# One core's encoder block: another order in the opening, output weights split a stage earlier, one slot more in the recurrence

## The chip, the cores and the metric

The kernel runs on one core of a Trainium2 chip. A core has five engines with a queue of instructions each: TensorE (PE in the profile; its weight loads are listed as PEld), VectorE (DVE), ScalarE (ACT), GpSimd (POOL) and SyncE (SP, which here only issues DMAs; ScalarE issues some too). An engine runs its instructions in the order of its queue and waits at one whose input is not there yet. PE writes into PSUM, eight banks of 128 x 512 floats; the others read the banks and work in the core's memory, SBUF. The metric is the device time of one execution in microseconds (us), the median of several runs.

## The reference

One layer of a bidirectional encoder on 1024 tokens of width 1024, all in float32:

```python
h = layer_norm(x, ln_in_g, ln_in_b)
proj = h @ w_in[l]
aq, ak, av, hq, hf_fwd, hf_bwd, hi, hg, ga, gh = jnp.split(proj, split_idx, axis=-1)
att = dilated_attention(aq, ak, av, slopes)
rec = hgrn2(hq, hf_fwd, hf_bwd, hi, hg, lower_bounds[:, l], hgrn_norm_g[l])
merged = jax.nn.sigmoid(ga) * (att @ w_att_up[l]) + jax.nn.sigmoid(gh) * (rec @ w_hgrn_up[l])
h = layer_norm(DEEPNORM_ALPHA * h + merged @ w_o[l], ln1_g[l], ln1_b[l])
gate, up = jnp.split(h @ w_ffn_in[l], 2, axis=-1)
h = layer_norm(DEEPNORM_ALPHA * h + (jax.nn.silu(gate) * up) @ w_ffn_out[l], ln2_g[l], ln2_b[l])
```

The projection has 11,776 columns, the feed-forward 2 x 2,816. The recurrence `hgrn2` is a gated linear one with 8 heads of 128 in both directions, in chunks; the attention has 24 heads of 64 in three groups with different dilation.

## The kernel before

**Products.** Every float32 operand is split into a high part (a cast to PE's fp32r type, on ScalarE, L212) and a low part (operand minus high part, on GpSimd or VectorE, L222). A product is three matmuls, high x high, high x low and low x high (`mm3`, L268 to L272), of 128 x 128 weights and 512 columns. The projection and the feed-forward use a scheme of Winograd's form of Strassen's method: tokens and contraction are halved, and seven products (numbers 1, 2, 6, 5, 7, 3, 4 in this order) with sums of weight blocks (`a11` to `a22`, `s1` to `s4`) and of activation blocks take the place of eight. The activation blocks are called `b11`, `b21` (first four token tiles) and `t1`, `t2`, `t3`, `b22`, `t4` (which need the other four): `t1 = b12 - b11`, `t2 = b22 - t1`, `t3 = b22 - b12`, `t4 = b21 - t2`. One product of one group is 12 matmuls of 512 columns; this is a slot of the projection.

**The order.** A planner with a model of the engines' times puts the instructions of each engine in order when the program is built, by priority (program order, raised by `high_priority`) and by when it thinks operands are ready. `behind` and `ordered` add an order between two instructions by hand. SP's loads of weight blocks are in a chain of their own (`queued`).

**Opening (`phase0`, L316 to L488).** The eight token tiles of x are loaded; VectorE takes the statistics (`stats`), GpSimd ends them, ScalarE normalises each half of a tile (`norm`), PE turns it 128 columns at a time into a bank (`turn`, L364), and ScalarE and VectorE apply gain and bias and write the blocks (`scaled`, `less`, `hi`, `lo`). Between the steps `run` lets `stream` (L615) issue the next slot of the projection. Four banks, used in turn (`ps_sd`), serve the turned tiles and some of the first products. `b22` is first kept as a scaled copy `w22`, and `t3` and `t4` come from GpSimd's subtractions (L467, L482).

**Projection with side work (`phase1`).** `stream` runs 23 groups of columns, 14 slots each. In each slot it prepares weights three slots ahead (`prep`) and the sums of weight blocks five slots ahead (`sums`, L652 to L657); results leave the banks through `plain`, `tanhs` and `silu2`. Beside it runs a generator of recurrence heads (`hgrn_side`) and attention units; the number it yields is the count of slots until its next piece. The recurrence masks its scores into two buffers (`hgrn_scores`, L1196 and L1197), adds them on GpSimd into `ham` (L1199, L1200), and multiplies them by the values two slots later (`hgrn_out`, L1217). A negative number also lets the next unit's loads begin.

**Up-projections and output projection (`phase2`).** Eight steps with the attention output and `w_att_up`, eight with the recurrence output and `w_hgrn_up`, each splitting its own weights. Chunks 0 to 3 of `w_o` are split within the second eight, chunks 4 to 7 after them (`wo_chunk`). Then come eight token tiles: product with `w_o`, first half and second half, residual, layer norm, turning, and the activation blocks of the feed-forward (`rest`, `h1_blocks`). `b22`, `t3` and `t4` go out to DRAM and come back whole. After the eighth tile's products PE runs the first two products of three feed-forward groups, then product 5, which needs `t1`.

The rest (feed-forward, its output product, last norm) keeps its form. SBUF is almost full all through: names such as `hi`, `st` or `wraw` given as `tag` are places that tiles share in turn, `bufs` is their number.

Of the kernel before, what the change touches and what calls it, by code (L numbers as in the profile page):

```python
# [79 lines left out]
class Block:  # L80
    evac_ahead = 1000

    def __init__(self, ctx, tc, x, ln_in_g, ln_in_b, w_in, hgrn_lb, hgrn_norm_g, w_att_up, w_hgrn_up,
# [15 lines left out]
        self.pad(self.cst, CST_PAD)  # L99
# [23 lines left out]
    def pad(self, pool, n):  # L123

        if n:
            self.nc.gpsimd.memset(pool.tile([128, n // 4], F32, name=f"pad{n}"), 0.0)
# [83 lines left out]
    def split(self, hi, lo, src, eng_hi="act", eng_lo="pool", key=None):  # L210
# [9 lines left out]
        self.cast = ins.ins.name  # L220
# [15 lines left out]
    gone = gone2 = None  # L236
# [19 lines left out]
    def weights(self, w, r0, nk, c0, pool=None, bufs=2):  # L256

        nc, wp = self.nc, pool or self.wp
        raw = self.wraw.tile([128, nk, 128], F32, name="w_raw", tag="wraw", bufs=bufs)
# [35 lines left out]
    def transposed(self, pool, n, q, g, b, v=None, bufs=2, on_act=(1, 3, 6)):  # L295

        nc = self.nc
        ps = self.ps_sd()
        for k in range(4):
            nc.tensor.transpose(ps[:, 128 * k:128 * (k + 1)], n[:, 128 * (4 * q + k):128 * (4 * q + k + 1)],  # L300
                                self.ident)
        if v is None:
            v = pool.tile([128, 4, 128], F32, name="tsv", tag="tsv", bufs=bufs)
        for k in range(4):
            kk = 4 * q + k
            p = ps[:, 128 * k:128 * (k + 1)]
            if kk in on_act:
                nc.scalar.activation(v[:, k, :], p, AF.Identity, bias=b[:, kk:kk + 1], scale=g[:, kk:kk + 1])
            else:
                nc.vector.tensor_scalar(v[:, k, :], p, g[:, kk:kk + 1], b[:, kk:kk + 1], op0=OP.mult, op1=OP.add)  # L310
        return v
# [4 lines left out]
    def phase0(self, pool, work):  # L316
# [8 lines left out]
        w11, t1, w22, z2 = (lent(z) for z in ("xb22hi", "xt3hi", "xt4hi", "xt4lo"))  # L325
        w21 = [self.half("v21") for _ in range(4)]

        strict = True

# [29 lines left out]
        def turn(tt, q, ks=range(4)):  # L359

            for k in ks:
                if tt % 4 == 0:
                    banks[k] = self.ps_sd()
                nc.tensor.transpose(banks[k][:, 128 * (tt % 4):128 * (tt % 4) + 128],  # L364
                                    xs[tt][:, 128 * (4 * q + k):128 * (4 * q + k) + 128], self.ident)
# [12 lines left out]
        def less(o, k, q, w):  # L378

            dve(nc.vector.scalar_tensor_tensor(o[k], banks[k], column("gin", 4 * q + k), w[k], op0=OP.mult,  # L380
                                               op1=OP.subtract))
# [32 lines left out]
        bias = [[column("bin", 4 * q + k) for k in range(4)] for q in range(2)]  # L414
        scaled(w11, 0, 0, True)
# [11 lines left out]
        norm(3, 1)  # L427
        stats(4)
        self.gates = [None] * 2 + [h.ins.name] * 2
# [11 lines left out]
        for tt in range(4, 8):  # L441
            norm(tt, 0)
            if tt < 7:
                stats(tt + 1)
            norm(tt, 1)
        run(3)
        for k in (0, 2):
            for tt in range(4, 8):
                turn(tt, 0, (k, k + 1))
            for i in (k, k + 1):  # L450
                less(t1, i, 0, w11)
            run()
        for k in (0, 2):
            for tt in range(4, 8):
                turn(tt, 1, (k, k + 1))
            for i in (k, k + 1):
                less(z2, i, 1, t1)
            for i in (k, k + 1):
                h = hi("t2", i, z2, bias[1][i]), lo("t2", i, z2, bias[1][i])
                scaled(w22, i, 1, True)  # L460
# [5 lines left out]
        for k in range(4):  # L466
            self.behind(nc.gpsimd.tensor_sub(w11[k], z2[k], w11[k]), last.ins.name)  # L467
# [1456 lines left out]
```

## Time and profile before

| | us |
|---|---|
| median of 3 runs | 2062.42 (2061.17 to 2066.87) |
| profiled execution, device time | 2064.15 |
| its span, first to last instruction | 2062.3 |
| PE busy | 2015.5 |
| VectorE busy | 1326.1 |
| GpSimd busy | 1063.9 |
| ScalarE busy | 947.6 |

How to read the rows. A row of waits has who waited on which line, for whom, then the total in us, the number and the longest. A group of instructions has line, engine, operation, written tile, read tiles and shape, the count after "x", then busy us and mean ns of one, then the engine's idle time just before them with what ended it. A row of the timeline has start, length, engine, line, operation, tiles, and the idle time before it in brackets. Matmuls overlap, so a row's length holds its latency; the distance of two starts is what one costs in a stream. `xt1hi` is the high part of `t1`, `w_lo` the low part of a weight block, `pj` and `sd` are banks, `wo1` the second four chunks of `w_o`.

### The profile page before, as it was taken

To read this page: it belongs to the slowest core of one execution; us is meant where nothing else is said; L and a number is where in the kernel's file an instruction comes from. 1 tells how busy PE (TensorE), PEld (TensorE's weight loads), DVE (VectorE), ACT (ScalarE), POOL (GpSimd) and SP (SyncE) were. 2 spreads that over 40 slices of the span, in tenths; PEclk is the share of its full clock that TensorE was granted. 3 is DMA by queue.
4 is the path that set the end of the run, shared out by engine and by line. 5 is a ranking of instruction groups with operands and counts; after the bars stand their busy time and mean duration, and the time that the engine had idled before them with its cause. 6 is when DMAs were issued, how large, how long until landed. Compare 5 with 4: busy or idle time off the path is not lost. (4 is left out here: it accounts for less than half of the span.)

```text
span 2062.3 us, 30940 instructions
## 1 busy us (share of the span) xinstructions
PE 2015.5 (98%) x10974; PEld 1670.5 (81%) x10974; DVE 1326.1 (64%) x2029; ACT 947.6 (46%) x1962; POOL 1063.9 (52%) x913
## 2 busy tenths in 40 slices
PE   7899999999999999999999999999999999999998
PEld 5688888788888888888888888787888888888886
DVE  6867645884377844677443225547777777767788
ACT  6554455553555536555365432244433333344541
POOL 5767644676446663666535652244656666630000
PEclk9999999999999999999999999999999999999999
DMA  5434533335334353344524376544544344358533
GB/s 158 133 115 142 171 119 105 128 129 177 116 127 132 114 177 98 121 131 145 165 95 150 123 247 204 183 133 125 171 131 141 127 149 137 108 170 298 160 96 128
DMA packets 274843, 297.94 MB, mean 144 GB/s; under 512 B 14017, under 2 KB 207362, under 8 KB 274690
## 3 DMA queue, kind: packets, MB, share of 16 engines
q1 hardware_dynamic: 268384, 274.78, 41.6%
q10 hardware_dynamic: 6306, 21.20, 2.7%
q8 instruction: 86, 1.41, 0.3%
q14 instruction: 67, 0.55, 0.1%
HBM read 201.29 MB, written 94.63 MB: 143 GB/s over the span
## 5 line engine op out<-in xcount | busy, mean ns | idle before, releaser
L222 POOL TENSOR_TENSOR w_lo<-wa,w_hi 128x512 fp32r<-128x512 f32 x272 | 362.6, 1341 | 274.7 <-ACT w_hi L212 259.7
L212 ACT CAST w_hi<-wa 128x512 fp32r<-128x512 f32 x272 | 168.4, 620 | 253.5 <-PE pj L271 146.8
L222 POOL TENSOR_TENSOR w_lo<-wsum,w_hi 128x512 fp32r<-128x512 f32 x88 | 128.0, 1464 | 111.7 <-PE sd L272 60.7
L222 POOL TENSOR_TENSOR w_lo<-f_raw,w_hi 128x512 fp32r<-128x512 f32 x66 | 102.5, 1561 | 53.2 <-ACT w_hi L212 51.8
L208 POOL TENSOR_TENSOR mv<-mv,mhalf 128x1 f32<-128x1 f32 x16 | 12.7, 797 | 218.9 <-DVE mv L207 218.1
L212 ACT CAST w_hi<-wsum 128x512 fp32r<-128x512 f32 x88 | 54.7, 621 | 122.2 <-PE sd L271 118.7
L542 DVE TENSOR_TENSOR evh<-wkeep,pj 128x512 f32<-128x512 f32 x45 | 30.9, 686 | 111.9 <-PE pj L272 63.2
L212 ACT CAST gwsum<-a_raw 128x512 fp32r<-128x512 f32 (+1 forms) x78 | 48.2, 618 | 112.6 <-PE pj L271 56.1
L270 PE MATMUL pj<-xt1hi,w_hi 128*128 128x512 f32 x252 | 99.6, 395 | 0.0
L270 PE MATMUL pj<-xb22hi,w_hi 128*128 128x512 f32 x252 | 99.1, 393 | 0.0
L272 PE MATMUL pj<-xb22hi,w_lo 128*128 128x512 f32 x252 | 98.2, 390 | 0.4 <-POOL w_lo L222 0.3
L271 PE MATMUL pj<-xb22lo,w_hi 128*128 128x512 f32 x252 | 98.6, 391 | 0.0
L272 PE MATMUL pj<-xt1hi,w_lo 128*128 128x512 f32 x252 | 98.5, 391 | 0.0
L271 PE MATMUL pj<-xt1lo,w_hi 128*128 128x512 f32 x252 | 98.4, 391 | 0.0
L654 POOL TENSOR_TENSOR wa<-wa,wa 128x512 f32<-128x512 f32 x46 | 67.1, 1467 | 40.4 <-DVE wa L653 35.5
L222 POOL TENSOR_TENSOR w_lo<-ws,w_hi 128x512 fp32r<-128x512 f32 x46 | 62.4, 1358 | 43.3 <-ACT w_hi L212 43.0
L680 ACT COPY wkeep<-pj 128x512 f32<-128x512 f32 x136 | 79.3, 583 | 7.8 <-PE pj L272 5.7
L531 DVE TENSOR_TENSOR evh<-wkeep,pj 128x512 f32<-128x512 f32 x66 | 57.8, 879 | 35.6 <-PE pj L272 25.1
L272 PE MATMUL pj<-xt2hi,w_lo 128*128 128x512 f32 x192 | 76.1, 396 | 4.1 <-POOL w_lo L222 4.1
L270 PE MATMUL pj<-xt2hi,w_hi 128*128 128x512 f32 x192 | 76.4, 401 | 1.1 <-ACT w_hi L212 1.1
L270 PE MATMUL pj<-xt4hi,w_hi 128*128 128x512 f32 x192 | 76.1, 396 | 0.8 <-ACT w_hi L212 0.8
L270 PE MATMUL pj<-xb11hi,w_hi 128*128 128x512 f32 x192 | 76.9, 402 | 0.0
(419 smaller groups left out, 6546.5 us busy)
## 6 DMA issues: line engine op xcount, KB each, us to landing
wa<-in_w_in_dram SPq DMA_DIRECT2D x184, 256.0 KB, 3.3
f_raw<-in_w_ffn_in_dram SPq DMA_DIRECT2D x44, 512.0 KB, 4.2
a_raw<-gd SPq DMA_DIRECT2D x30, 512.0 KB, 3.7
gd<-fc SPq DMA_DIRECT2D x44, 256.0 KB, 2.1
gd<-fs SPq DMA_DIRECT2D x33, 256.0 KB, 2.1
tg<-evh SPq DMA_DIRECT2D x32, 256.0 KB, 2.2
tg<-tg SPq DMA_DIRECT2D x16, 512.0 KB, 3.9
y<-ahs SPq DMA_DIRECT2D x16, 512.0 KB, 6.5
```

What stands on the lines that cost most here:

```text
L208: nc.gpsimd.tensor_tensor(mv[:, 2:3], mv[:, 2:3], self.mhalf[:, 0:1], OP.pow)
L212: ins = nc.scalar.copy(hi, src) if eng_hi == "act" else nc.vector.tensor_copy(hi, src)
L222: ins = e.tensor_sub(lo, src, hi.bitcast(F32))
L270: nc.tensor.matmul(ps, whi, xhi, start=first, stop=False, **kw)
L271: nc.tensor.matmul(ps, whi, xlo, start=False, stop=False, **kw)
L272: self.product = nc.tensor.matmul(ps, wlo, xhi, start=False, stop=last, **kw).ins.name
L531: self.left(nc.vector.tensor_tensor(o, self.order_src(add, g, kind), s, OP.add))
L542: self.left(nc.vector.tensor_add(t, add, ps))
L654: nc.gpsimd.tensor_sub(a["a21"], a["a22"], a["a11"])
L680: nc.scalar.copy(t, ps)
```

## The change

Three groups of edits, made together.

1. **Opening.** Before the first four tiles' turns PE turns the identity 11, 7, 6 and 4 times into a corner of a bank that is overwritten later (`run_up`). The second halves of tiles 1 to 3 and the first halves of tiles 6 and 7 are normalised on VectorE. The casts of the first two weights stand behind the normalisations of tiles 1 and 2. The first weight sums of product 6 are put off (`later`). `t3` comes from a kept copy `w12` and a bank; `b22` is written from the bank; the subtraction for `t4` is VectorE's.
2. **Slot.** `hgrn_side` yields -3 instead of -2 between scores and outputs, the sums into `ham` have priority, and gates at even places of the list are summed in their bank instead of in SBUF. The loads of the attention output after the last unit stand 4 slots apart instead of 6.
3. **Output weights and last tiles.** Each step of the second up-projection splits the next step's weights and one chunk of `w_o`; chunks 4 to 7 go where the attention output lay. `t1` and `t3` of the feed-forward come from a kept scaled copy `w11` and the bank. The last tile's `b22` and `t3` are split straight into their place; only the first 384 columns of each come back from DRAM, `b22` ahead of the last tile's norm (`spread`). The last tile's norm is halved over two engines. Gates of the first three feed-forward groups are formed one product later.

```diff
+        WARM = (11, 7, 6, 4)
         def norm(tt, q):
             x, mv = xs[tt][:, HALF * q:HALF * (q + 1)], self.mv0[:, tt, :]
+            if tt > 5 and q == 0 or 0 < tt < 4 and q:
+                return dve(nc.vector.tensor_scalar(x, x, mv[:, 2:3], mv[:, 3:4], op0=OP.mult, op1=OP.add))
             return act(x, x, AF.Identity, bias=mv[:, 3:4], scale=mv[:, 2:3])
...
+        def run_up(n):
+
+            for i in range(n):
+                if 3 not in banks:
+                    banks[3] = self.ps_sd()
+                ins = nc.tensor.transpose(banks[3][:, 384:512], self.ident, self.ident)
+                if i == 0 and self.turned_last:
+                    self.behind(ins, self.turned_last)
+                self.turned_last = ins.ins.name
...
+        self.gates = [None] * 2
         for tt in range(4):
-            norm(tt, 0)
+            n = norm(tt, 0)
+            if 0 < tt < 3:
+                self.gates[tt - 1] = n.ins.name
+            run_up(WARM[tt])
             turn(tt, 0)
             if tt < 3:
                 stats(tt + 1)
+            if tt == 0:
                 norm(tt, 1)
+        for tt in range(1, 4):
+            norm(tt, 1)
...
             for i in (k, k + 1):
-                less(t1, i, 0, w11)
+                scaled(w12, i, 0, True)
+                self.left(less(t1, i, 0, w11))
+            if k == 0:
+                for z in self.later:
+                    z()
+                self.later = None
             run()
...
+            for i in (k, k + 1):
+                ins = less(w12, i, 1, w12)
+                if i > k:
+                    self.behind(ins, parts[0][1].ins.name)
+                g, b, z = column("gin", 4 + i), bias[1][i], self.xb["b22"][0][:, i, :]
+                self.behind(act(z, banks[i], AF.Identity, bias=b, scale=g), h[0].ins.name)
+                act(hb[i], z.bitcast(F32), AF.Identity, bias=nbin[:, i:i + 1])
+                dve(nc.vector.scalar_tensor_tensor(self.xb["b22"][1][:, i, :], banks[i], g, hb[i], op0=OP.mult,
+                                                   op1=OP.subtract))
...
-        for k in range(4):
-            self.behind(nc.gpsimd.tensor_sub(w11[k], z2[k], w11[k]), last.ins.name)
...
-            self.behind(nc.gpsimd.tensor_sub(w21[k], w21[k], z2[k]), last.ins.name)
+            self.behind(nc.vector.tensor_sub(w21[k], w21[k], z2[k]), last.ins.name)
```

```diff
     def silu2(self, dst, odd):
-                x = add
+                x = add if odd else ps
                 nc.vector.tensor_add(x, add, ps)
...
         am = self.half3("ham")
-        nc.gpsimd.tensor_add(am[N_, :, N_], self.amx[N_, :, N_], self.amy[N_])
-        nc.gpsimd.tensor_add(am[F_, :, F_], self.amx[F_, :, F_], self.amy[F_])
+        with self.tc.high_priority(offset=self.evac_ahead):
+            nc.gpsimd.tensor_add(am[N_, :, N_], self.amx[N_, :, N_], self.amy[N_])
+            nc.gpsimd.tensor_add(am[F_, :, F_], self.amx[F_, :, F_], self.amy[F_])
...
         am = [self.hgrn_scores(st, b) for b in range(2)]
-        yield -2
+        yield -3
```

```diff
+            ahead = next_weights(0)
+            next(rs)
+            split = None
             for d in range(8):
                 t = tgate(8 + d)
+                ws = ahead
+                if d < 7:
+                    ahead = next_weights(d + 1)
                 next(rs)
+                if d == 1:
+                    wo.append([self.ap.tile([128, KT, HALF], F32R, name=f"wo1{n}", tag=n, bufs=1) for n in ("hi", "lo")])
+                if split:
+                    split()
+                c = d // 2 + 4 * (d % 2)
+                split = self.wo_chunk(wo, c)
...
-            for c in range(4, 8):
-                self.wo_chunk(wo[1], c, "dve")
...
                     if t == 7:
-                        nc.vector.tensor_scalar(y, y, mv[:, 0:1], mv[:, 2:3], op0=OP.subtract, op1=OP.mult)
+                        nc.vector.tensor_scalar(y[:, 0:HALF], y[:, 0:HALF], mv[:, 0:1], mv[:, 2:3], op0=OP.subtract,
+                                                op1=OP.mult)
+                        self.normalise(yp, y[:, HALF:D], y[:, HALF:D], mv)
...
         def later(i, name, v):
-            nc.sync.dma_start(self.td[i][:, :, c], v)
+            if t == 7 and i < 2:
+                put(name, v)
+            else:
+                nc.sync.dma_start(self.td[i][:, :, c], v)
...
         t1, t2 = tmp(), tmp()
-        b12 = v(0)
-        less(t1, b12, 0, "b11")
-        b22 = v(1)
+        ps = self.transposed(y, 0)
+        for k in range(4):
+            ins = nc.vector.scalar_tensor_tensor(t1[:, k, :], ps[k], gc[:, k:k + 1], w11[k][:, c], op0=OP.mult,
+                                                 op1=OP.subtract)
+        self.t1_last = ins.ins.name
+        b22 = scaled(1, self.transposed(y, 1), (0, 1, 2, 3) if t < 7 else (0, 2))
+        put("t1", t1)
```

More of the change, by code (lines that the diff above doesn't have):

```diff
@@ L234, in ordered @@
         return ins
-    gone = gone2 = None
+    gone = gone2 = later = None
     def left(self, ins):
@@ L440, in phase0 @@
         strict = False
[L441 to L445, printed above, removed]
+        for tt in range(5, 8):
+            stats(tt)
+        for q in range(2):
+            for tt in range(4, 8):
+                norm(tt, q)
+        self.later = []
         run(3)
@@ L648, in sums @@
             a = A[g]
+            if n == 0 and p == 6 and self.later is not None and not again:
+                self.later.append(lambda: sums(i, True))
+                return
             with early(n):
@@ L1399, in follow @@
                 self.ffn_pools()
[L1400 removed]
+                for n, tag in (("b22", "hi"), ("t3", "lo")):
+                    t = self.ap.tile([128, 2, 4, HALF], F32R, name=f"x{n}", tag=tag, bufs=1)
+                    self.xb[n] = [t[:, i] for i in range(2)]
+                self.again = {n: self.ffn_again(n, 384) for n in ("b22", "t3")}
+                self.spread("b22")
             def rest(t, y):
@@ L1501, in h1_blocks @@
         later(1, "t3", t3)
-        later(0, "b22", b22)
-        if then:
-            then()
         t4 = tmp()
```

244 lines of the change are left out of this document (147 added, 97 removed).

## The prediction

> **What bounds the kernel now.** I read the head of the page first, then who waited for whom on TensorE (PE) in three stretches, then the granted clock around the long waits, and last the queues of the other engines where a wait ends.
>
> ```profile
> span 2062.3 us, 30940 instructions
> PE 2015.5 (98%) x10974; PEld 1670.5 (81%) x10974; DVE 1326.1 (64%) x2029; ACT 947.6 (46%) x1962; POOL 1063.9 (52%) x913
> ```
>
> PE is busy 98% of the span and the change removes no product, so the time can only fall where PE waits or runs slowly. The next rows give PE's waits (total, times, longest) from 17 to 100 us (opening), from 100 to 1270 us (projection with attention and recurrence beside it) and from 1270 to 1450 us (second up-projection, output projection).
>
> ```profile
> PE sd L271 <- DVE xt1lo L390: 2.7, 2, 2.4
> PE sd L364 <- DVE evh L542: 2.0, 1, 2.0
> PE pj L272 <- POOL w_lo L222: 2.0, 2, 1.0
> PE pj L270 <- ACT w_hi L212: 1.9, 2, 1.1
> PE sd L271 <- DVE xb22lo L391: 1.9, 3, 0.7
> PE sd L270 <- DVE lent_xt3hi L380: 0.8, 1, 0.8
> ...
> ```
>
> ```profile
> PE sd L1217 <- POOL ham L1200: 3.5, 2, 2.3
> PE pj L272 <- POOL w_lo L222: 3.1, 3, 2.1
> ...
> ```
>
> ```profile
> PE pj L270 <- ACT wo1hi L212: 2.4, 1, 2.4
> PE pj L272 <- POOL w_lo L222: 2.0, 3, 0.9
> PE sd L270 <- ACT xt1hi L212: 2.0, 1, 2.0
> PE pj L271 <- DVE wo1lo L222: 0.5, 1, 0.5
> ```
>
> A wait of about 2 us is followed by a stretch in which PE is granted half its clock. The windows view shows it: after the window come its length, PE's busy time (with its instructions), the other engines', then the clock.
>
> ```profile
> 38.10:44.90 6.80, 5.96 (x17) 4.36 (x16) 3.19 (x6) 1.22 (x3) 4.15 (x4) 0.50 0.10 39
> 62.00:65.40 3.40, 3.05 (x8) 1.94 (x7) 3.20 (x10) 1.47 (x3) 0.84 (x5) 0.50 0.91 261
> 393.10:396.50 3.40, 3.40 (x11) 2.72 (x10) 3.18 (x6) 2.63 (x9) 1.82 (x2) 0.50 0.21 77
> 908.50:911.90 3.40, 3.40 (x18) 3.40 (x17) 0.18 (x1) 2.80 (x6) 3.01 (x4) 0.50 0.02 5
> 1335.20:1338.60 3.40, 2.95 (x7) 2.38 (x8) 1.69 (x3) 0.00 (x0) 0.00 (x0) 0.50 0.87 250
> 1441.00:1444.40 3.40, 3.40 (x10) 2.62 (x9) 3.37 (x3) 0.00 (x0) 2.15 (x2) 0.50 0.85 277
> ```
>
> Half of PE's busy time in such a window is lost: 3.0, 1.5, 1.7, 1.7, 1.5 and 1.7 us. I charge each loss to the wait ahead of it.
>
> **The change part by part: the opening.** Start first.
>
> ```profile
> 12.18 0.26 POOL L353 TENSOR_SCALAR mv<-mv 128x1 f32<-128x1 f32 x1
> ```
>
> ```profile
> 13.69 0.81 ACT L331 ACTIVATE xt<-xt,mv 128x512 f32<-128x512 f32 x1
> ```
>
> ```profile
> 14.56 2.79 PE L364 MATMUL sd<-tabs_sb,xt 128*128 128x128 f32 x10 [0.81 <-ACT xt L331]
> ...
> 17.00 1.20 PE L270 MATMUL pj<-xb11hi,w_hi 128*128 128x512 f32 x2
> ...
> 19.92 0.63 PE L271 MATMUL pj<-xb11lo,w_hi 128*128 128x512 f32 x1
> 20.35 0.63 PE L272 MATMUL pj<-xb11hi,w_lo 128*128 128x512 f32 x1
> ...
> 23.08 0.39 PE L272 MATMUL pj<-xb11hi,w_lo 128*128 128x512 f32 x1
> 23.30 0.39 PE L270 MATMUL pj<-xb11hi,w_hi 128*128 128x512 f32 x1
> ```
>
> The fourth tile's statistics stand at 12.44 (12.18 plus 0.26), but ScalarE reaches its normalisation at 13.69, as it also does the second halves of tiles 1 and 2 and two weight casts. The change gives those halves to VectorE, behind its statistics, and holds the casts behind normalisations 1 and 2: 1.2 us earlier (13.69 less 12.44), so the first product starts near 15.8 instead of 17.00. Products start 0.43 us apart at 20 us (20.35 less 19.92) and 0.22 apart at 23 us: half clock again, from 17.00 to about 21, or nine products with 0.2 us lost in each: 1.8 us. The 28 added transposes of the identity fill PE's waits before the first product; I take it that they make the clock rise by then. Unknown cost, bounds 0 and 1.8 us of gain; I take 1.8, since the windows above link half clock to idle PE.
>
> [...] No run here has a long stretch of transposes alone to settle it.
>
> Then come the second four tiles. The wait on `evh` (2.0) is PE waiting for a bank whose evacuation is queued on VectorE behind the first weight sums; those now go behind the first two subtractions (`later`). With the `lent_xt3hi` wait (0.8) and its half clock (3.0) that is 5.8 us. The other waits, `xt1lo` 2.7 plus 1.5, `xb22lo` 1.9, `w_hi` 1.9, `w_lo` 2.0, make 10.0. All that PE could win in the opening is 1.2 + 1.8 + 5.8 + 10.0 = 18.8 us. But a PE that comes earlier meets VectorE:
>
> ```profile
> L391 DVE SCALAR_TENSOR_TENSOR xb22lo<-lent_xt4hi,vc,xb22hi 128x512 fp32r<-128x512 f32 x4 | 5.9, 1531 | 0.0
> L390 DVE TENSOR_TENSOR xt1lo<-lent_xt3hi,xt1hi 128x512 fp32r<-128x512 f32 x4 | 5.8, 1493 | 0.0
> L391 DVE SCALAR_TENSOR_TENSOR xt2lo<-lent_xt4lo,vc,xt2hi 128x512 fp32r<-128x512 f32 x4 | 5.0, 1265 | 0.1
> ...
> L380 DVE SCALAR_TENSOR_TENSOR lent_xt4lo<-sd,vc,lent_xt3hi 128x512 f32<-128x512 f32 x4 | 2.8, 743 | 0.0
> ...
> L556 DVE TENSOR_TENSOR wkeep<-wkeep,sd 128x512 f32<-128x512 f32 x3 | 2.1, 685 | 3.8 <-PE sd L272 3.8
> ```
>
> ```profile
> L467 POOL TENSOR_TENSOR lent_xb22hi<-lent_xt4lo,lent_xb22hi 128x512 f32<-128x512 f32 x4 | 6.4, 1636 | 0.0
> L482 POOL TENSOR_TENSOR v<-v,lent_xt4lo 128x512 f32<-128x512 f32 x4 | 5.5, 1410 | 0.0
> ```
>
> The same shape costs VectorE 0.74 us from a bank (L380) and 1.3 to 1.5 us from SBUF while GpSimd works. The change takes L467 and L482 off GpSimd. Up to the end of `xt1lo` VectorE loses its idle 3.8 us (it waited for the slow PE) and, with `xt2lo` and `xt1lo` at 0.75 each, 10.8 less 6.0 = 4.8 us; it gains four subtractions for `w12` and four `xb22lo` that now come first, 8 x 0.74 = 5.9 us. Net 2.7 us earlier, and 3.0 us (1.2 + 1.8) more if PE hands it the banks that much sooner. I take 5.7 of the 13.0 us (1.2 + 1.8 + 5.8 + 4.2) up to there. The half clock at the first `t1` product stays, as PE still waits there. Behind it `xb22lo` is long done: 1.9 us. The `w_hi` and `w_lo` waits stand behind a GpSimd that no longer has L482, but also behind weight loads and the first recurrence unit, which stay: half, 2.0 us. The four subtractions of L482 on VectorE (at most 4 x 1.5 = 6.0 us) have 24 `t1`, 24 `t3` and 24 `b22` products to hide under, 72 x 0.23 = 16.6 us; uncovered, they cost up to 6.0. **Opening: 9.6 us**, bounds 0 and 18.8.
>
> **The slot between scores and outputs.** PE waits 3.5 us for `ham`, GpSimd's sum of the masked scores, twice, once with a half clock behind it (window 908.5, 1.7 us).
>
> ```profile
> 906.86 0.72 POOL L1200 TENSOR_TENSOR ham<-amx,amy 64x256 f32<-64x256 f32 x1
> ```
>
> One slot is 12 products, 12 x 0.23 = 2.8 us, longer than the longest wait (2.3). **Gain 5.2 us.** The eight more slots come out of the idle slots at the end of the projection, where the loads of the attention output are also pulled together. Two edits go with it: the four sums (0.72 each) jump ahead of weight splits on GpSimd, and some gates are summed in their bank, which then stays held for a tanh and one VectorE operation more; the next writer of that bank is three products, 8.3 us, away. I put the bank edit at 0.
>
> The longer unit shifts every later unit against the products, so waits born of chance meetings of queues are drawn anew: those for `w_lo` (3.1, longest 2.1 with the 1.7 us window at 393.1) may vanish or come twice. Bounds: a gain of 4.8, a loss of 4.8. I take a loss of 3.8, one more wait of the longest kind.
>
> **Output weights and last tiles.** Chunks 4 to 7 of `w_o` are now split one per step of the second up-projection, into the buffers of the attention output. This removes 2.4 + 0.5 us and the half clock of window 1335.2 (1.5): 4.4 us. The up-projection's weights are split a step ahead, which removes `w_lo`, 2.0 us. SP now has a residual load that waits for a row buffer ahead of the `w_o` load; a whole step of 48 products, 11 us, covers it.
>
> At the last token tile PE waits 2.0 us for `xt1hi`, plus 1.7 (window 1441).
>
> ```profile
> 1425.83 1.78 DVE L1407 TENSOR_SCALAR y<-y,mv 128x1024 f32<-128x1024 f32 x1
> ...
> 1435.57 1.50 DVE L1489 TENSOR_TENSOR tsum<-tsv,xb11hi 128x512 f32<-128x512 f32 x1
> 1437.10 0.69 DVE L1490 TENSOR_TENSOR tsum<-tsum,xb11lo 128x512 f32<-128x512 f32 x1
> ```
>
> The normalisation is halved over two engines (0.9 us saved) and the two subtractions (2.2 us) fall away, as `t1` comes straight from the bank: 3.1 us, more than the 2.0. Against that, the split of `b22` is put ahead of the tile: two subtractions of 768 columns, near 1.0 us each by the 0.69 of 512. If both got into the chain, 1.1 us of the 3.1 would be left. I take the full 3.7. That the tile's share of `b22` and `t3` no longer goes out to DRAM and back, and that the first three gates of the feed-forward are put off, takes work from the same stretch, where no other wait is left to win: 0. **Gain 10.1 us**, bounds 4.4 and 10.1.
>
> **Sum.** 9.6 + 5.2 + 10.1 - 3.8 = 21.1 us. The profiled execution took 2064.15 us for its span of 2062.3, and the median of the runs is 2062.42; the forecast goes from the median: **2041 us**.
>
> **The rivals.**
> 1. *VectorE keeps the pace of the opening.* For it: it has no idle time from 50 to 60 us (the third pair in this row of the windows view is VectorE's), and the change gives it eight operations that GpSimd did or that came later. Then the opening gives 0: 2051 us. Against it: the 3.8 us idle and the slowdown beside GpSimd.
>
> ```profile
> 50.00:60.00 10.00, 9.24 (x41) 7.22 (x39) 10.00 (x10) 7.06 (x14) 9.26 (x7) 1.00 0.07 26
> ```
>
> 2. *The identity transposes do not raise the clock.* The loss is 1.8 us: 2043 us. The ten transposes from 14.56 us on did not raise it by 20.35, which speaks for it; they were broken by waits, which speaks against. [...]
> 3. *The sums of the scores hold up the weight splits (slower).* Both halves of a head put 4 x 0.72 = 2.9 us on GpSimd at high priority, ahead of `w_lo`. If a split is then late by that and the clock halves behind it (1.7), a head costs 4.6 us. It makes the kernel slower from six of eight heads on (27.6 against the 21.1); with all eight, 2041 + 37 = 2078 us. Against it: splits are made three products (8.3 us) ahead.
> 4. *The waits only move.* PE comes earlier everywhere and meets the same producers: 2060 us, within the noise. Against it: the waits ahead of the windows at 908, 1335 and 1441 us end on work that is shortened or moved ahead, not on a full engine.
> 5. *No new wait and all of the opening:* 2062.4 - 18.8 - 15.3 = 2028 us.
>
> **How the numbers follow.** Forecast 0.50; rival 1 0.18; rival 2 0.14; rival 3 0.07; rival 4 0.07; rival 5 0.04. The range 2026 to 2060 holds all but rival 3 and some of rival 4. A difference of 0.3%, 6 us, is about what can be told from no change: faster than 2056 is the forecast, rivals 1 (most of it), 2 and 5: 0.84; the same is rival 4 and a little of 1: 0.08; slower is rival 3 and an unseen cost of its size: 0.08.
>
> **What would show it.** First product near 15.8 us and 0.23 us apart from there; no half-clock window at 38 us; the `evh` and `xb22lo` rows gone; no L1217 wait on `ham`; no `wo1hi` or `xt1hi` wait, no half clock near 1335 and 1441. Wrong it would be if the engines' rows after show new PE waits on `w_lo` in the projection over 6 us, or a VectorE wait of over 5 us before the first `t1` product.

## The result, and the profile after

| | median us | range, runs | ratio to before | 95% interval |
|---|---|---|---|---|
| before | 2062.14 | 2061.17 to 2066.87, 6 | 1 | |
| changed | 2049.35 | 2046.21 to 2053.33, 6 | 0.9939 | 0.9929 to 0.9950 |

The change saves 12.8 us, 0.6%, where 21.1 were forecast. The profiled execution was the fastest of the six (2046.21 us, span 2044.4). It stands 17.9 us below the profiled one of before (2064.15), so this pair of traces shows some 5 us that most executions don't have. For that reason the changed kernel was profiled a second time (`changed_again` below, 2051.47 us).

The head of the page, changed kernel:

```profile
span 2044.4 us, 31027 instructions
PE 2008.2 (98%) x11002; PEld 1667.9 (82%) x11002; DVE 1315.3 (64%) x2065; ACT 945.4 (46%) x1964; POOL 1053.9 (52%) x906
```

PE's busy time fell by 7.3 us though it has 28 more instructions: products at half clock count as longer busy time (0.43 us from one to the next near 20 us before, 0.22 at full clock), and there are fewer of them: the mean granted clock is 0.998 here and 0.993 in the profile of before. PE's waits, in the same three stretches as before (total, times, longest), the first from 17 to 100 us:

```profile
PE pj L274 <- POOL w_lo L224: 3.0, 4, 1.4
PE pj L273 <- DVE xt2lo L402: 1.7, 2, 1.0
PE sd L272 <- DVE lent_xt3hi L391: 1.5, 1, 1.5
PE sd L362 <- ACT xt L326: 1.2, 1, 1.2
PE sd L362 <- DVE evh L597: 0.6, 1, 0.6
...
PE sd L273 <- DVE xt1lo L401: 0.4, 1, 0.4
```

From 100 to 1270 us, and from 1270 to 1450 us:

```profile
PE pj L274 <- POOL w_lo L224: 3.4, 4, 1.2
PE pj L272 <- DVE mT L1418: 1.6, 1, 1.6
PE pj L272 <- DVE evh L597: 1.2, 1, 1.2
...
```

```profile
PE sd L273 <- DVE xt1lo L224: 2.2, 1, 2.2
```

The waits for `ham`, `wo1hi`, `wo1lo`, `xt1hi` and `xb22lo` are gone. `xt2lo`, `mT`, a wait on `evh` in the projection (1.2 us) and, at the last tile, `xt1lo` are new, and `lent_xt3hi` rose from 0.8 to 1.5 us. The half clock of 38, 62, 393, 908 and 1335 us is gone too; two windows are left besides the last microseconds (after the window: length, busy time of PE, PEld, DVE, ACT, POOL, then the clock):

```profile
17.07:20.48 3.41, 3.41 (x13) 2.74 (x12) 2.88 (x5) 3.38 (x7) 0.54 (x1) 0.50 1.12 331
1423.36:1426.77 3.41, 3.41 (x10) 2.64 (x9) 3.41 (x9) 1.06 (x3) 0.00 (x0) 0.50 0.00 0
```

To see where the time went, the start of each product is set against the start of the same product in the trace of before. This table gives the median lead in us (positive is earlier than before) over the products that start, in the trace of before, in the 20 us from the time at the head of the column: 140 us is behind the opening, 1200 behind the projection, 1320 behind the second up-projection but ahead of the old `wo1hi` wait, 1360 behind that wait and 1460 behind the last tile. The differences between the columns are the stages' gains. The kernels of the lower lines come in the next section.

```
                                       140    1200    1320    1360    1460
changed, first profile                6.45   13.53   12.08   16.93   17.75
changed_again                         5.43   10.64    6.79   11.65   12.48
open_alone                            2.53    9.47   12.36   15.68   15.03
slot_alone                           -1.16    0.06    2.49    2.76    2.91
wo_alone                             -1.57   -0.72   -7.94   -3.08   -0.85
opening_and_slot                      5.75   10.40   12.15   12.70   12.20
wo_and_residual_order                 0.07    1.66    4.55    9.40   10.51
split_behind_norm                     8.43   13.36   11.15   16.00   18.24
split_behind_norm_no_warmup           5.52   10.41    5.28   10.14   12.28
t3_behind_t1                          6.65   10.59    7.79   12.64   14.77
weights_before_residual               4.46    9.79   12.67   17.53   19.77
norm_and_residual                     5.98    9.82   12.70   17.56   18.66
all_three                             5.89   12.80   15.69   20.54   22.82
```

Three kernels keep the opening of before. They stand between -1.6 and 0.1 in the first column, and the projection adds 0.8 to 1.6 us in them, though only one of them has an edit that bears on it (the slot). Differences of about 1.5 us in these two columns may therefore be chance. The `wo1` stage, 1320 to 1360, is 4.9 us in every kernel that has the edit. Without the edit it is 0.3 us in `slot_alone`, 0.6 in `opening_and_slot`, but 3.3 in `open_alone`: that wait, too, shrinks at times by itself. In `open_alone` the projection also adds 6.9 us with no edit of the slot, as much as in the changed kernel.

For the changed kernel the stages read, in its two profiles: opening 6.5 and 5.4, projection 7.1 and 5.2, up-projection -1.5 and **-3.9**, the `wo1` wait 4.9 and 4.9, the last tile 0.8 and 0.8. The second sum, 12.5, is the one that agrees with the medians.

**Why the up-projection loses.** ScalarE and VectorE there, in the first profile, between the rows of PE that wait for them:

```profile
1217.28 1.23 DVE L539 SCALAR_TENSOR_TENSOR a<-a,ginb 128x1024 f32<-128x1024 f32 x1 [9.13 <-ACT a L538]
1218.42 0.68 DVE L1418 SCALAR_TENSOR_TENSOR mT<-tg,pj 128x512 f32<-128x512 f32 x1
...
1219.25 0.47 PE L272 MATMUL pj<-rec_hi,w_hi 128*128 128x512 f32 x1 [1.58 <-DVE mT L1418]
...
1264.72 1.25 ACT L538 ACTIVATE a<-a,mv 128x1024 f32<-128x1024 f32 x1 [4.79 <-DMA a<-in_x_dram]
1265.87 0.60 ACT L214 CAST w_hi<-w_raw 128x512 fp32r<-128x512 f32 x1
...
1266.52 0.50 PE L272 MATMUL pj<-rec_hi,w_hi 128*128 128x512 f32 x1 [0.71 <-ACT w_hi L214]
1268.40 0.51 PE L274 MATMUL pj<-rec_hi,w_lo 128*128 128x512 f32 x1 [1.15 <-POOL w_lo L224]
```

The residual's row (L538, L539) stands ahead of a weight cast on ScalarE and of an eviction on VectorE, and its data is not there yet. ScalarE idles 4.79 us for the load, and the cast behind L538 in its queue comes 1.15 us after it, at 1265.87 us; the eviction on VectorE (1218.42 us) stands in the same way behind L539, ahead of which VectorE idles 9.13 us. In before, too, casts stood behind such rows, but the rows came one to a step of 11 us. Now the load of a row is issued a row ahead into one of two buffers, and ScalarE has the eight rows between 1216.01 and 1264.72 us, 7.0 us apart: as fast as the loads come, with a wait at nearly each. Two rows of before, for comparison:

```profile
1255.98 1.25 ACT L499 ACTIVATE a<-a,mv 128x1024 f32<-128x1024 f32 x1 [5.96 <-DMA a<-in_x_dram]
...
1268.51 1.25 ACT L499 ACTIVATE a<-a,mv 128x1024 f32<-128x1024 f32 x1 [7.22 <-DMA a<-in_x_dram]
```

**Why the opening starts no earlier.** GpSimd, ScalarE and PE in the first profile:

```profile
12.45 1.27 POOL L224 TENSOR_TENSOR w_lo<-wa,w_hi 128x512 fp32r<-128x512 f32 x1
...
13.81 0.27 POOL L348 TENSOR_SCALAR mv<-mv 128x1 f32<-128x1 f32 x1
...
14.12 0.81 ACT L326 ACTIVATE xt<-xt,mv 128x512 f32<-128x512 f32 x1 [1.51 <-POOL mv L348]
...
14.98 0.66 PE L362 MATMUL sd<-tabs_sb,xt 128*128 128x128 f32 x4 [1.74 <-ACT xt L326]
...
16.94 1.09 PE L272 MATMUL pj<-xb11hi,w_hi 128*128 128x512 f32 x2
```

The fourth tile's statistics end with L348 on GpSimd, and a weight split of 1.27 us has slipped ahead of it. PE waits 1.74 us, and the half clock follows at 17.07. The start also moves with a load: in the second profile the statistics of the second tile wait for x until 8.02 us (6.75 in the first), and the first product starts at 18.26 us.

**Why the last tile gains little.** VectorE and PE:

```profile
1412.64 0.95 DVE L224 TENSOR_TENSOR xb<-t_raw,xb 128x768 fp32r<-128x768 f32 x1
...
1417.23 3.86 DVE L224 TENSOR_TENSOR xt<-t_raw,xt 128x768 fp32r<-128x768 f32 x2
...
1421.33 0.68 DVE L224 TENSOR_TENSOR xt1lo<-tsum,xt1hi 128x512 fp32r<-128x512 f32 x1
...
1422.06 0.50 PE L273 MATMUL sd<-xt1lo,w_hi 128*128 128x512 f32 x1 [2.21 <-DVE xt1lo L224]
```

The split of `t3` (`xt`, two subtractions of 768 columns) stands ahead of `xt1lo` and takes 3.86 us. The split of `b22` (`xb`) is out of the way by then; its two subtractions took 0.94 and 0.95 us.

### The profile page after: what moved, and what is told of

Read it like the earlier page. It is cut to its first block, busy times and chain, and to the rows that moved or that the text cites. A ratio compares the mean times of both kernels' runs of the same rounds, so it can differ in the third digit from the quotient of the medians.

```text
span 2044.4 us, 31027 instructions
## 1 busy us (share of the span) xinstructions
PE 2008.2 (98%) x11002; PEld 1667.9 (82%) x11002; DVE 1315.3 (64%) x2065; ACT 945.4 (46%) x1964; POOL 1053.9 (52%) x906
## 5 line engine op out<-in xcount | busy, mean ns | idle before, releaser
L273 PE MATMUL pj<-xt2lo,w_hi 128*128 128x512 f32 x192 | 75.5, 393 | 1.7 <-DVE xt2lo L402 1.7
L224 DVE TENSOR_TENSOR gwkeep<-a_raw,gwsum 128x512 fp32r<-128x512 f32 (+1 forms) x78 | 53.1, 681 | 36.3 <-ACT gwsum L214 33.5
L273 PE MATMUL pj<-xb11lo,w_hi 128*128 128x512 f32 x192 | 76.0, 397 | 0.0
L274 PE MATMUL pj<-xt4hi,w_lo 128*128 128x512 f32 x192 | 75.1, 391 | 0.7 <-POOL w_lo L224 0.7
```

What stands on the lines that cost most here:

```text
L224: ins = e.tensor_sub(lo, src, hi.bitcast(F32))
L273: nc.tensor.matmul(ps, whi, xlo, start=False, stop=False, **kw)
L274: self.product = nc.tensor.matmul(ps, wlo, xhi, start=False, stop=last, **kw).ins.name
```

## The experiments

The first four take the change apart on the kernel before; the others edit the changed kernel. Where nothing else is said, the kernel before ran on the same chip.

**`open_alone`, `slot_alone`, `wo_alone`**: each group of edits by itself on the kernel before. For the first:

```diff
+            run_up(WARM[tt])
...
+            for z in self.later:
```

> Edits of the opening alone, the rest as before. The stage shifts of the two traces give the opening 6.5 us (median shift of the same PE instructions at 140 to 200 us) and the projection behind it another 7.1. Theory A, the parts add up and the 7.1 belong to the slot: 6.5 us less than before, the ham waits of 3.5 us still there. Theory B, the 7.1 are waits born of chance meetings that any shift draws anew: somewhere between 0 and 13 us less, and a ham wait that differs from 3.5. The first product near 17 us in both.

For the second:

```diff
-        yield -2
+        yield -3
...
+        with self.tc.high_priority(offset=self.evac_ahead):
```

> Edits of the slot alone (yield of 3, priority of the sums into ham, gates summed in the bank, loads of the attention output 4 slots apart). Theory A: the ham waits (3.5 us) and the half clock behind one of them (1.7) go, 5.2 us less than before, and the wait for w_lo near 389 us with its half clock (2.1 and 1.7) stays, as nothing ahead of it differs. Theory B: new waits in the projection, total between 5 less and 5 more. Rival 3 of the prediction: w_lo waits of PE in the projection above 6 us.

For the third:

```diff
-            a = pool.tile([128, D], F32, name="a0", tag="st", bufs=4)
+            rows.append(pool.tile([128, D], F32, name="a0", tag="row", bufs=2))
...
+            ahead = next_weights(0)
```

> Edits of the second up-projection, output weights and last tiles alone. By the traces of the whole change: wo1 waits and half clock gone (4.9 us), but a wait of 1.6 us on mT before the second up-projection and 0.7 + 1.2 us on weights inside it in place of the 2.0 us before, and a wait of 2.2 us on xt1lo with its half clock where 2.0 us on xt1hi stood. Theory A: 4 us less than before in the total. If the prediction's term were right and the waits came from the other parts, 10 us less.

| | median us | before, same chip | ratio | 95% interval |
|---|---|---|---|---|
| opening alone | 2054.32 | 2060.44 | 0.9976 | 0.9966 to 0.9987 |
| slot alone | 2061.05 | 2060.44 | 0.9999 | 0.9988 to 1.0011 |
| output weights alone | 2060.05 | 2060.44 | 0.9999 | 0.9985 to 1.0012 |

By these ratios the parts give 4.9, 0.2 and 0.2 us, 5.3 in all, and together they give 12.8. They don't add, so at least one of them depends on another. (`open_alone` was profiled in its fastest execution, 2049.2 us, 5 us under its median, and `wo_alone` in its slowest, 2065.87 us, 6 us above it: the first line of the table is better than most executions of its kernel, the second worse.) For the opening both theories are left standing: 4.9 us, by the interval 2.7 to 7.0, and the `ham` waits stayed, at 2.8 us. The 5.2 us expected of the slot and the 4 of the output weights did not come. Slot alone, PE's waits from 100 to 1200 us:

```profile
PE pj L272 <- POOL w_lo L222: 7.3, 4, 3.2
```

The 3.5 us for `ham` are gone and `w_lo` has risen from 3.1 to 7.3: the gain is taken back by waits for weight splits on GpSimd. Two waits make up most of it, 3.2 us to 392.25 and 3.1 us to 884.00 us. GpSimd ahead of the second:

```profile
879.41 1.21 POOL L1110 TENSOR_SCALAR t<-t,gna,ga 128x1024 f32<-128x1024 f32 x1
880.58 1.19 POOL L1123 TENSOR_TENSOR t<-t,fb 128x512 f32<-128x512 f32 x1
881.72 2.23 POOL L222 TENSOR_TENSOR w_lo<-wa,w_hi 128x512 fp32r<-128x512 f32 x1
```

What stands ahead of the splits there are the first operations of a recurrence unit (at 392 us such operations and sums of weight blocks), not the sums into `ham`: none of those runs in the 30 us ahead of either wait. Output weights alone, PE's waits from 1200 to 1345 us, with half clock from 1267.7 (3.4 us) and from 1284.8 us (6.8 us):

```profile
PE pj L272 <- POOL w_lo L222: 2.3, 2, 1.1
PE pj L270 <- ACT w_hi L212: 2.3, 2, 1.4
```

The `wo1` waits are gone here too (the lead rises by 4.9 from 1320 to 1360 us), but 7.2 us are lost ahead of them in this execution.

**`opening_and_slot`**: both groups on the kernel before, without the third.

> The opening and the slot on the kernel before, without the output weights' edits. Theory A, that the parts' gains simply add: 4.9 and 0.2 us, a ratio of 0.997 to 0.998, and near 2055 us; the output weights' edits then give 7 us that they do not give alone. Theory B, that the slot pays once the opening has moved TensorE and GpSimd against each other (the opening alone still shows a wait of 2.5 us for ham at 897 us, the slot alone two of 3.1 us for weight splits at 389 and 881 us): a ratio of 0.995 to 0.996, no wait for ham, and under 4 us of waits for weight splits in the projection.

Measured: 2051.18 us against 2063.11, ratio 0.9945 (0.9931 to 0.9960), 11.3 us; theory B, but for a ratio just under its range. That is nearly all that the whole change gives (0.9939, and 0.9942 in the next run). So by the ratios the slot pays beside the opening, some 6 us (0.9976 of `open_alone` less 0.9945, of 2062; 1 to 11 us by the ends of the two intervals, and the two ran on different chips), and the third group adds about one, which can't be told from nothing. PE's waits from 100 to 1200 us have no `ham`, and `w_lo` is back to where it was before:

```profile
PE pj L274 <- POOL w_lo L224: 3.6, 3, 2.3
```

By which queue the opening helps the slot the profile doesn't say, and no edit was tried for it. The leads don't show it either: the projection adds 4.7 us here and 6.9 in the one profile of `open_alone`, its fastest execution. That is left open.

**`changed_again`**: the changed kernel, unedited, timed beside the next three.

> The changed kernel itself, unedited, as the standard beside the others. Ratio to the kernel before 0.993 to 0.995 (0.9939 so far). Its first profile fell on the fastest of its six executions (2046.2 us). Theory A, that a wait of TensorE of 2 to 3 us for a weight split on GpSimd near 871 us, with a half clock behind it, is the usual case (it stands in three of four profiles of kernels next to it): this profile shows it, and a span of 2047 to 2050 us. Theory B, that those kernels brought it: no such wait here, and a span near 2044.4 us.

Measured: 2051.13 us against 2063.11, ratio 0.9942 (0.9926 to 0.9959). The profile has the wait near 871 us, as three kernels next to it have, and its span is 2049.7 us, both as theory A said. PE's wait from 860 to 890 us, then GpSimd and ScalarE ahead of it, then the window:

```profile
PE pj L274 <- POOL w_lo L224: 2.3, 1, 2.3
```

```profile
865.28 0.81 ACT L1150 ACTIVATE fa<-t,gb,ga 128x504 f32<-128x504 f32 x1 [4.42 <-DMA t<-hg6t]
...
866.92 2.46 POOL L1152 TENSOR_SCALAR t<-t,gna,ga 128x1024 f32<-128x1024 f32 x1 [0.40 <-ACT fb L1151]
...
870.68 1.19 POOL L1165 TENSOR_TENSOR t<-t,fb 128x512 f32<-128x512 f32 x1
871.84 2.21 POOL L224 TENSOR_TENSOR w_lo<-wa,w_hi 128x512 fp32r<-128x512 f32 x1
```

```profile
875.64:879.05 3.41, 3.41 (x10) 2.63 (x9) 3.41 (x3) 0.62 (x1) 3.41 (x4) 0.50 0.65 205
1223.80:1227.21 3.41, 3.41 (x9) 2.65 (x9) 1.95 (x3) 1.75 (x2) 0.97 (x1) 0.50 0.66 141
```

A unit of the recurrence starts when its gather lands. In the first profile of the same program it landed 2.6 us earlier (862.72 us, next row), while PE was only 1.0 us ahead. PE then waited 1.0 us at the split, with no half clock. So the difference between the profiles, and much of the spread of 7 us between executions, may well be the landing time of a transfer; it was seen, not tested by an edit.

```profile
862.72 0.81 ACT L1150 ACTIVATE fa<-t,gb,ga 128x504 f32<-128x504 f32 x1 [2.88 <-DMA t<-hg6t]
```

**`split_behind_norm`, `split_behind_norm_no_warmup`**: the weight splits on GpSimd wait for the fourth tile's statistics; in the second the 28 identity transposes are left out as well.

```diff
+            ins = nc.gpsimd.tensor_scalar(mv[:, 3:4], mv[:, 0:1], mv[:, 2:3], -1.0, op0=OP.mult, op1=OP.mult)
+            if tt == 3:
+                self.mv_done = ins.ins.name
...
+            self.behind(ins, self.mv_done)
```

```diff
-        WARM = (11, 7, 6, 4)
+        WARM = (0, 0, 0, 0)
```

> The whole change, and in the opening GpSimd's first weight splits ordered behind the statistics of tile 3. In the trace of the change a split of 1.27 us stands ahead of the last of them, ScalarE normalises tile 3 at 14.12 instead of 12.7, PE waits 1.7 us and its clock, at full since 10.2 us, is halved from 17.07 to 20.48. Theory A, the forecast's start was right and only this split was in its way: first product near 15.5 us (16.94 in the change), full clock from there, 3.2 us ahead of the change at 27 us. What is left of that at 140 us tells whether VectorE paces the rest: 3 us if not, under 1 us if it does.

> As split_behind_norm, but none of the 28 transposes of the identity. Theory A, transposes count as activity for the clock: without them the clock is at half until about 19 to 21 us, products 0.43 us apart, and at 27 us this run is 1.5 to 2 us behind split_behind_norm. [...]

Measured: 2048.16 us, ratio 0.9929 (0.9914 to 0.9943), and 2052.18, ratio 0.9948 (0.9933 to 0.9963), before 2063.18. The wait at 13 us shrinks, and the first product starts at 15.71 us, where the forecast had put it:

```profile
13.76 0.66 PE L366 MATMUL sd<-tabs_sb,xt 128*128 128x128 f32 x4 [0.41 <-ACT xt L328]
...
15.71 0.70 PE L274 MATMUL pj<-xb11hi,w_hi 128*128 128x512 f32 x2
```

The opening is 2.0 us ahead of the changed kernel's first profile (8.43 against 6.45), and the projection takes it back (13.36 against 13.53): this profile has the late split at 871 us. By the ratios the edit's worth can't be told from nothing.

With the transposes the clock rises earlier. Four turns of a tile's 128 columns, without the identity transposes and with them:

```profile
12.37 1.11 PE L366 MATMUL sd<-tabs_sb,xt 128*128 128x128 f32 x4 [2.19 <-ACT xt L328]
```

```profile
12.30 0.60 PE L366 MATMUL sd<-tabs_sb,xt 128*128 128x128 f32 x4
```

Over all profiles the clock is first granted in full at 20.4 to 21.8 us in the five without the identity transposes, and at 8.8 to 15.5 us in the nine with them. The medians of this pair are 4.0 us apart (2045.93 to 2049.99 against 2051.40 to 2052.44), though the intervals of the ratios overlap. The leads after the opening are 2.9 apart, but not all of that is the clock: in the kernel without the transposes the second tile's load also landed later (its statistics start at 8.29 us, 6.72 in the other). The half clock itself, 3.2 us from the first product (18.22 us) to 21.42, is worth half of that, 1.6 us by estimate.

**`t3_behind_t1`**: VectorE splits `t3` only when `t1`'s low part is done.

```diff
-        self.t1_last = ins.ins.name
...
-        put("t1", t1)
+        self.t1_last = put("t1", t1).ins.name
```

> The whole change, with VectorE's split of the reloaded part of t3 (two operations, 3.9 us) ordered behind the low part of t1 of the last tile, not only behind t1 itself. Theory A: PE's wait of 2.2 us on xt1lo and the half clock behind it (1.7) go, 3.9 us less between 1400 and 1460 us, and nothing later, as t3 is used some products on. Theory B: the chain of the last tile is too long all the same, and a wait of 1 to 2 us stays.

Measured: 2051.30 us, ratio 0.9946 (0.9931 to 0.9960): no gain in time. PE's waits there:

```profile
PE sd L272 <- ACT wkeep L1646: 1.0, 1, 1.0
PE sd L272 <- DVE wkeep L1736: 0.6, 1, 0.6
...
```

The `xt1lo` wait and its half clock are gone, and waits for `wkeep` stand in their place, the longest at 1459 us: ScalarE and VectorE move or add a product's result there from its bank (L1646, L1736), and PE waits for them. The last tile gains 2.1 us instead of 0.8. But kernels without this edit whose wait of 1.9 us happened to draw no half clock gain 2.2 there as well (`split_behind_norm`, `weights_before_residual`), so by these traces the edit is worth at most the 1.3 us of a half clock that comes now and then.

**`weights_before_residual`**: the residual's first instructions on ScalarE and VectorE go behind the last weight cast and the last `mT` eviction in program order.

```diff
-            nc.scalar.activation(a, a, AF.Identity, bias=mv[:, 3:4], scale=mv[:, 2:3])
-            nc.vector.scalar_tensor_tensor(a, a, ALPHA, gb, op0=OP.mult, op1=OP.mult)
+            self.behind(nc.scalar.activation(a, a, AF.Identity, bias=mv[:, 3:4], scale=mv[:, 2:3]), self.cast)
+            self.behind(nc.vector.scalar_tensor_tensor(a, a, ALPHA, gb, op0=OP.mult, op1=OP.mult), self.mt_last)
```

> The whole change, with ScalarE's step of the residual ordered behind the weight casts of its step, and VectorE's behind the last evacuation of the first up-projection. In the change both stand ahead of these and wait for the load of x (5 to 10 us). Theory A: the waits of 1.6 us on mT, 0.7 on w_hi and 1.2 on w_lo go, 3.5 us less between 1200 and 1300 us against the trace of the change. Theory B, the loop of two row buffers (load, three operations, store) is itself too slow for a step of 11 us: the wait moves to the residual's own reader or to a later weight load, under 1 us less.

Measured: 2044.22 us, ratio 0.9910 (0.9893 to 0.9926). No wait of PE is left from 1200 to 1340 us, and the stage goes from a loss to a gain of 2.9 us. The rows are one to a step again, 10.9 us apart (1254.44, then 1265.33 us), without a wait for their load, and each stands right behind a cast:

```profile
1264.80 0.62 ACT L214 CAST w_hi<-w_raw 128x512 fp32r<-128x512 f32 x1 [2.10 <-PE pj L273]
1265.33 1.24 ACT L538 ACTIVATE a<-a,mv 128x1024 f32<-128x1024 f32 x1
```

**`wo_and_residual_order`**: the same edit on `wo_alone`, to see whether the residual was what kept the third group at nothing.

> The output weights' edits on the kernel before (as in wo_alone), with the residual's scaling on ScalarE put behind the weight cast in program order and its first product on VectorE behind the first mT tiles. Theory A, that wo_alone came out even only because the residual, waiting for its load, held up the casts and evictions queued behind it on ScalarE and VectorE: the loss of 9.7 us at 1240 to 1280 us goes to under 2 us, wo1 and the last tile keep their 4 to 5 and 1 to 3 us, and the ratio is 0.996 to 0.9975 (5 to 8 us faster than before). Theory B, that the conversions and splits of wo1 moved into the up-projection cost what they save: the loss stays above 5 us, the ratio 0.999 to 1.001.

Measured: 2054.46 us against 2061.70, ratio 0.9963 (0.9950 to 0.9977), 7.6 us, where the same kernel without the edit gave 0.9999. Theory A holds: the up-projection goes from -7.2 to +2.9 us (the first in an execution 6 us above the median, so the ratios are the better measure).

**`norm_and_residual`, `all_three`**: the edits together, without and with that of `t3_behind_t1`.

> Two edits together: the weight splits behind tile 3's statistics, and the residual behind the weight casts of the up-projection. Theory A, that the two gains stand in different stages and add: the opening gains 2.0 us, the up-projection 2.5 us, the ratio to the kernel before is 0.989 to 0.990 (2040 to 2042 us). Theory B, that what is gained in the opening is waited off again at 871 us, where GpSimd's recurrence hands over late: ratio 0.991, as with the residual alone, with a wait over 2 us near 871 us in the profile.

> The two edits of norm_and_residual and the third tiles' split behind the first product's low part. Theory A, that the third edit only trades one wait at 1420 us for others (copies of kept weights 1.6 us): the same time as norm_and_residual within 1 us. Theory B, that the wait of 2.2 us and the half clock at 1423 us go and nothing comes: 2 to 3 us faster than norm_and_residual.

Measured, against 2063.11: 2043.35 us, ratio 0.9904 (0.9888 to 0.9921), and 2042.34 us, ratio 0.9903 (0.9886 to 0.9920). Both save some 20 us and beat the changed kernel beside them (0.9942; their slowest run, 2045.39 us, is below its fastest, 2047.90). The residual's order gives nearly all of what they gain over it: alone, on another chip, it had 0.9910. The other two edits can't be told from nothing in these times. For `norm_and_residual` the ratio lies between the two theories; its profile has the wait near 871 us that B names (2.0 us, with a half clock), while that of `all_three`, with the same opening, has not. For `all_three` the time is as theory A had it, 1.0 us from the other; the "copies of kept weights" in that expectation are the results in `wkeep`.

## Why the prediction was right, and where it was not

The direction and the range held; the forecast of 2041 us was 8 us too low. That 2049 is almost the time of rival 1 (2051) is chance: rival 1 had the opening at 0, and the opening gave 5.4 and 6.5. That it is no more than 8 us is luck in part, too: in the second profile opening, up-projection and last tile fell short by 4.2, 5.9 and 2.9 us, and the projection gave 3.8 us more than was put down for it.

- **Start and clock of the opening** (1.2 + 1.8). The statistics were ready in time in the forecast, 15.8 us for the first product. They ended at 14.08 us in place of 12.44, because a weight split got ahead of their last instruction on GpSimd: the prediction moved casts on ScalarE and did not ask where the splits behind them would land. The idea was right (with the split held back the statistics end at 12.86 us and the first product starts at 15.71). With the identity transposes the clock was granted in full at 10.24 us, ahead of the first product, so rival 2 fell. But the full clock was lost again from 17.07 us, behind PE's wait of 1.74 us, so little of the 1.8 us came in that profile (3.41 us at half clock behind the first product, 4.04 before).
- **The second four tiles** (2.7 net from VectorE, 1.9, 2.0). `xb22lo` went as said; `evh` fell from 2.0 to 0.6, and the windows at 38 and 62 us went (one at 39 us came back in other profiles). VectorE sets the pace as forecast, now with `xt2lo` (1.7). But `lent_xt3hi`, which was to go, rose to 1.5 us, and `w_hi` and `w_lo` together fell from 3.9 to 3.0 us, less than the 2.0 put down for them. Forecast 9.6, measured 5.4 and 6.5.
- **The slot** (5.2, less 3.8 for new waits). `ham` is gone, as forecast. The charge of 3.8, a guess at one more chance wait, comes near what `w_lo` rose by in the slot by itself, 4.2 us. Beside the opening `w_lo` stayed at its old level (2.3 and 3.2 us against 3.1), and the stage gave 7.1 and 5.2 in place of 1.4; how much of that is the slot's stays open, as `open_alone` shows. `slot_alone` has the prediction's sign of being wrong, `w_lo` over 6 us in the projection, but not by rival 3: no sum for `ham` stands ahead of its two long waits. The bank edit, put at 0, may cost something: a wait of 1.2 us on `evh` (L597, the last read of a gate's bank) is new. It isn't in `slot_alone`, which has that edit too, and no run takes the edit by itself.
- **Output weights** (2.0 + 4.4). The wait and half clock of `wo1` were worth 4.9 us, in every kernel that has the edit, against 4.4 in the forecast. The step that failed is this one: "SP now has a residual load that waits for a row buffer ahead of the `w_o` load; a whole step of 48 products, 11 us, covers it." It looked at who is queued behind that load on SP, and not at who is queued behind the *instruction that needs it* on ScalarE and VectorE: the weight casts and the evictions. The stage lost 1.5 and 3.9 us where 2.0 of gain were forecast; with the order mended it gained 2.9. (Some of that 2.0 was not the edit's: the `w_lo` waits of before shrink or vanish in the kernels that don't have it as well, and those gain 1.8 to 2.9 us in this stage.) This is the largest miss, 3.5 and 5.9 us in the two profiles, and the run that mends it ends 3 us from the forecast.
- **Last tile** (3.7). The `xt1hi` wait went, and `xt1lo` came for it: 0.8 us. The prediction priced the two subtractions of `b22`, at 1.0 us each, and left them out of the chain; that was right (0.94 and 0.95 us). The two of `t3` it did not price at all: it saw in that edit only work taken from the stretch, at 0. They took 1.9 us each beside GpSimd's splits and stood in the chain.

The sum of the stages in the second profile: 5.4 + 5.2 - 3.9 + 4.9 + 0.8 = 12.5 us.

## What to carry to other kernels

When a load and its buffers are moved, follow it to the instruction that consumes it, and ask what stands behind that instruction in its engine's queue; a consumer that need not be early belongs behind the work that PE waits for. Where parts of a change share an engine's queue, time them in pairs as well as alone: here two parts that gave 4.9 and 0.2 us gave 11.3 together, and a third one gave nothing until two instructions were put later in their queues. A gain read from one pair of traces can be off by the spread of the runs (12.5 and 17.8 us for the same kernel here, with a median of 12.8), so profile an execution near the median before terms are compared.

## What the runs showed of the hardware

- Waits of PE of 1.6 to 2.3 us are followed by a window of 3.41 us at half clock in some cases and not in others. In the changed kernel's first profile those of 1.74 us (to 14.98) and 2.21 us (to 1422.06) were, the one of 1.58 us (to 1219.25) was not; one of 1.9 us at the last tile of `weights_before_residual` was not either. Where a window of 3.40 or 3.41 us followed, it cost another 1.5 to 1.7 us by estimate, half of PE's busy time in it (2.95 to 3.41 us in the profiled windows of before and after). No run was made to find what decides between the two.
- With the turns of the identity the clock is granted in full at 10.24 us in the changed kernel, 6.7 us ahead of its first product; without them, in the one before, at 21.04 us, 4.0 us behind it (first profiles).
- VectorE's normalisation of 128x512 took 0.54 us (11.51 us in the changed kernel) and 1.47 us (14.12 us), the second beside a subtraction on GpSimd that began at 14.04 us. The two rows:

```profile
11.51 0.54 DVE L353 TENSOR_SCALAR xt<-xt,mv 128x512 f32<-128x512 f32 x1
...
14.12 1.47 DVE L353 TENSOR_SCALAR xt<-xt,mv 128x512 f32<-128x512 f32 x1 [2.06 <-POOL mv L348]
```
